# Prologue of a one-layer hybrid decoder: first loads on one queue in larger pieces, squares of x summed on GpSimd, the norm's product one group earlier

## The chip, the cores and the metric

The kernel runs on one core of one Trainium2 chip. The metric is the device time of one execution in microseconds. TensorE is called PE here, VectorE DVE, ScalarE ACT, GpSimd POOL and SyncE SP, as the profile does.

## The reference

One layer of a decoder trunk on x of 256 tokens by 1024 features, all float32:

```
xn   = rms_norm(x, attn_norm_g)              # x * rsqrt(mean(x*x) + eps) * g
proj = xn @ w_in                             # 1024 -> 3088 columns: q, k, v of 8 attention heads; q, k, v, r and a
                                             # 16-column gate of 4 gated-linear-attention heads
x    = x + concat(attention(rope(q), rope(k), v), gla(q', k', v', gate) * silu(r)) @ w_out
x    = x + ConvGLU(rms_norm(x))              # 1024 -> 2 x 2816, causal conv of 3 taps, silu gate, 2816 -> 1024
out  = rms_norm(x)
```

The first norm is what the change touches: the projection needs, for every token, one factor `rsqrt(mean(x*x) + eps)`.

## The kernel before, in words

x comes transposed, 128 features by 256 tokens in each of 8 k-tiles. Every float32 product is made of three reduced-precision ones: an operand is split into `hi` (rounded, by ACT, line 95) and `lo` (the rest, by DVE, line 98), and PE adds hi·hi, hi·lo and lo·hi. For x the two halves are `ah` (ACT, line 173) and `al` (DVE, line 174), multiplied with the norm's weight on the way; the norm's factor per token is left out and put in when a product is read back.

The projection runs in six groups of columns, "G" (gate and GLA q, k: 528 columns), then q, k, v, gv and r (512 each). A loop over q = 0 to 47 takes one k-tile of one group at a step: q 0 to 7 is group G, q 8 to 15 group q, and so on. In group G a step has three passes of four matmuls (line 671), with `hi,ah`, `hi,al` and `lo,ah`; in group q a step has 12 matmuls (lines 112 to 114). Everything else that ACT, DVE and SP do is hung on these steps by a table at line 587: the entry with number q is issued ahead of step q, one with q + 0.5 in its middle. On ACT, DVE and PE the order of issue is the order of the program; an instruction that waits holds all that stand behind it on its engine.

Weights come through four buffers `raw` ("slots"): slots 0 to 3 hold two k-tiles of group G each (`in_wG`, 528 KB a slot), slots 4 and 5 the two halves of group q (`in_w`, 1024 KB each, loaded in two pieces), and so on. When a slot's last `lo` is made, SP issues the load of the slot four further on. The kernel issues x in five pieces: k-tiles 0 and 1 from ACT's queue, 2-3, 4-5 and 6-7 from SP's, between the weights. A load takes one of eight completion semaphores in turn, and an issue waits until the load that had its semaphore before has landed.

The norm goes in these steps. `xsq(n)` squares two k-tiles (ACT, line 236). `xadd(n)` adds them up (DVE, line 239) and `xsum` makes one tile `s1` of 256 tokens (DVE, line 243). `xnorm` has PE sum `s1` over the partitions (line 250, ahead of the middle of step 8) and then makes the factor `rsx` with a Ln and an Exp on ACT (lines 181 and 182) and four small DVE instructions (lines 180 and 183 to 185). `g_evac` reads group G back with that factor (ACT, lines 266 and 267); `g_lr_split` splits its 16 gate columns (DVE, lines 278 and 279); `xrow` spreads the factor over a tile with PE (line 258) to scale cos and sin; `g_transpose_lr` and `g_transpose` transpose the read-back tiles on PE (lines 284 and 293).

Of the kernel before, what the change touches and what calls it, by code (L numbers as in the profile page):

```python
# [34 lines left out]
def trunk_kernel(ctx: ExitStack, tc: tile.TileContext, xT_d, wG_d, w5_d, wo_d, up_d, dn_d,  # L35
                 par_d, gla_g_d, fin_g_d, wgu_d, cos_d, sin_d, causal_d, lvl_d, ident_d, out_d):
    nc = tc.nc
# [13 lines left out]
        return ps_att.tile([128, 512], F32, name="att")  # L51


    par = const.tile([128, NPAR], F32, name="par")
    cos = const.tile([128, S], F32, name="cos")
    sin = const.tile([128, S], F32, name="sin")
# [91 lines left out]
    rsx = main.tile([128, 8], F32, name="rsx")  # L148

    slots[0].raw = ring.tile([128, 2048], F32, name="raw", bufs=RAW)  # L150
    def load_x(q, k0, k1):
        a, b = (KT + S * k0 if k0 else 0), KT + S * k1
        q.dma_start(xg[:, a:b], xT_d[:, a:b])


    with tc.manual_schedule(engines={mybir.EngineType.Activation}):
        load_x(A, 0, 1)
        load_x(A, 1, 2)
        A.preload_act_table_set("natural_log_exp_and_others")
    for a, b in ((0, 272), (272, NG), (NG, 2 * NG)):  # L160
        DMA.dma_start(slots[0].raw[:, a:b], slots[0].src[:, a:b])
    nload[0] = 1
    load_x(DMA, 2, 4)
    load_next()
    load_x(DMA, 4, 6)
    load_next()
    load_x(DMA, 6, 8)
    load_next()
    for dst, src in ((ident, ident_d), (cos, cos_d), (sin, sin_d), (par, par_d), (wgu, wgu_d)):
        DMA.dma_start(dst, src)  # L170
# [64 lines left out]
    def xsq(n):  # L235
        A.activation(xsqs[:, 2 * n:2 * n + 2], xT[:, 2 * n:2 * n + 2], AF.Square)

    def xadd(n):
        V.tensor_add(xsqs[:, 0:2], xsqs[:, 0:2], xsqs[:, 2 * n:2 * n + 2])

    def xsum():
        s1 = at.tile([128, S], F32, name="s1")
        V.tensor_add(s1, xsqs[:, 0], xsqs[:, 1])
        st["s1"] = s1
        st["mh"] = main.tile([128, KT, S], F32R, name="mh", tag="mh")

# [333 lines left out]
    def do(*fs):  # L580
        for f, *a in fs:
            f(*a)
# [1 line left out]


    for q, f in (
            (2, lambda: do((gsplit, 6), (xsq, 2), (xadd, 1), (gsplit, 7), (xsq, 3), (xadd, 2))),
            (4, lambda: do((hi, 4, 0), (lo, 4, 0), (xadd, 3), (xsum,), (hi, 4, 1), (lo, 4, 1))),
            (6, lambda: do((hi, 5, 0, 1),)),
            (8.5, lambda: do((xnorm,), (lo, 5, 0), (g_evac, 0), (g_evac, 1), (g_lr_split,), (hi, 6, 0), (lo, 5, 1))),  # L590
            (10, lambda: do((DMA.dma_start, lvl, lvl_d), (DMA.dma_start, causal, causal_d))),
            (10.5, lambda: do((xrow,), (g_wgs,))),
            (11, lambda: do((g_transpose_lr,), (g_transpose, 0), (g_transpose, 1), (lo, 6, 0), (g_diag,))),
            (12.5, lambda: do((g_gate_mm,), (g_gate,), (hi, 6, 1), (g_decay,), (lo, 6, 1), (hi, 7, 0))),
            (14, lambda: do((lvl_u, 0), (lo, 7, 0), (hi, 7, 1), (lvl_u, 1), (lo, 7, 1))),
            (16, lambda: do((rope_a, 0, 0), (rope_b, 0, 0), (rope_a, 0, 1), (rope_b, 0, 1), (hi, 8, 0), (lo, 8, 0), (hi, 8, 1), (lo, 8, 1))),
            (20, lambda: do((hi, 9, 0), (lo, 9, 0), (hi, 9, 1), (DMA.dma_start, glag, gla_g_d))),
            (24, lambda: do((lvl_first,), (lvl_u, 2), (rope_a, 1, 0), (rope_b, 1, 0), (rope_a, 1, 1), (rope_b, 1, 1), (lo, 9, 1), (hi, 10, 0), (lo, 10, 0), (g_diag2, 0), (g_diag2, 4))),
# [20 lines left out]
    def gsplit(k):  # L619
        sl, a = slots[k // 2], NG * (k % 2)  # L620
        if k % 2 == 0:
            sl.alloc()
        xsplit(k)
        if k == 1:
            xsq(0)
        sl.split(a, a + NG)

    slots[0].alloc()
# [4 lines left out]
    slots[0].split_lo(272, NG)  # L633
    for k in range(1, 5):
        gsplit(k)
    xsq(1)
    gsplit(5)

    def emit(q):
        for f, a in plan.get(q, []):  # L640
            f(*a)

    names = ["G", "q", "k", "v", "gv", "r"]
    for q in range(48):
        g, k = divmod(q, 8)
        emit(q)
        if k == 0:
            if g == 0:
                st["G"] = [(acc(), att()) for _ in range(2)]
            else:  # L650
                st[names[g]] = [acc() for _ in range(2)]
        if g == 0:
            h_, l_ = slots[k // 2].view(NG)
            kk = k % 2
        else:
            h_, l_ = slots[4 + 2 * (g - 1) + k // 4].view(512)
# [413 lines left out]
```

## Time and profile before

| | |
|---|---|
| median of 3 runs | 312.95 us (312.08 to 314.29) |
| profiled execution, its own time | 313.25 us |
| its span, first to last instruction | 311.3 us |
| PE busy | 303.0 us, 97% of the span |
| DVE, ACT, POOL busy | 79%, 65%, 1% of the span |
| DMA moved | 55.38 MB, mean 178 GB/s |
| mean granted TensorE clock | 0.996 |

The median is that of three timed runs; the profile is one more execution, whose time is 0.3 us above it. Busy time of PE says that matmuls are in flight; whether they follow each other without a gap is seen in the waits of PE and in the order of time.

### The profile page before, as it was taken

Reading aid. Unit: us, or ns where it says so; the run is one execution under the profiler, and the core shown is the slowest. Engines: PE = TensorE matmul, PEld = TensorE weight load, DVE = VectorE, ACT = ScalarE, POOL = GpSimd, SP = SyncE. Lnnn points to the kernel's source line nnn. Section 1 sums busy time; section 2 is a strip of 40 time slices with the busy share of each in tenths; the row PEclk is TensorE's granted clock in tenths of the full one; section 3 lists DMA queues with packets and bytes.
Section 4 is the critical chain, followed back from the end, with each engine's and each line's share of the span. In section 5 each row is a group of like instructions: output and inputs, shape, how many; then the busy total and the mean of one; then the engine's idle time right before and its main releaser. Section 6 shows DMA issues by size and latency. Waiting matters only on the chain.

```text
span 311.3 us, 6126 instructions
## 1 busy us (share of the span) xinstructions
PE 303.0 (97%) x2460; PEld 283.0 (91%) x2460; DVE 246.4 (79%) x455; ACT 201.0 (65%) x364; POOL 1.8 (1%) x12
## 2 busy tenths in 40 slices
PE   7999999999999999999999999999999999999992
PEld 7999997777789999999999999999999999999982
DVE  3879989988558497999999878788777777776653
ACT  5869997796967396467666655556666555534362
POOL 1000000000000000000000000000000000000000
PEclk9999999999999999999999999999999999999998
DMA  7998553543370725593566654445455722120003
GB/s 222 387 385 317 190 182 114 227 139 135 138 272 5 259 74 197 218 378 157 206 209 251 262 212 171 165 177 188 194 202 205 269 69 67 67 69 0 2 0 135
DMA packets 12155, 55.38 MB, mean 178 GB/s; under 512 B 1360, under 2 KB 2912, under 8 KB 7776
## 3 DMA queue, kind: packets, MB, share of 16 engines
q1 hardware_dynamic: 11696, 54.48, 47.9%
q10 hardware_dynamic: 432, 0.53, 0.6%
q8 instruction: 19, 0.31, 0.4%
q14 instruction: 8, 0.07, 0.1%
HBM read 53.95 MB, written 1.05 MB: 177 GB/s over the span
## 4 chain that ended last, share of the span: by engine, by line
PE 90%; DMA 6%; issue 1%; ACT 1%; DVE 1%; SPq 0%; DVEq 0%; ACTq 0%
PE att L114 14%; PE att L113 14%; PE att L112 14%; PE acc L112 14%; PE acc L113 14%; PE acc L114 14%; DMA raw<-in_w 2%; DMA raw<-in_wG 2%; DMA xg<-in_xT 1%; PE att L378 1%; PE att L541 1%; PE att L510 1%; PE att L556 1%; PE att L440 1%; PE acc L830 0%
## 5 line engine op out<-in xcount | busy, mean ns | idle before, releaser
L95 ACT ACTIVATE hi<-raw 128x1024 fp32r<-128x1024 f32 (+3 forms) x83 | 79.6, 977 | 52.2 <-PE att L113 43.1
L98 DVE TENSOR_TENSOR lo<-raw,hi 128x1024 fp32r<-128x1024 f32 (+3 forms) x86 | 93.8, 1099 | 11.9 <-ACT hi L95 11.8
L112 PE MATMUL att<-hh,hi 128*128 128x256 f32 x352 | 98.5, 280 | 0.0
L114 PE MATMUL att<-hh,lo 128*128 128x256 f32 x352 | 98.4, 279 | 0.0
L113 PE MATMUL att<-hl,hi 128*128 128x256 f32 x352 | 98.3, 279 | 0.0
L112 PEld LDWEIGHTS att<-hh,hi 128*128 128x128 f32 x352 | 66.2, 188 | 0.0
L114 PEld LDWEIGHTS att<-hh,lo 128*128 128x128 f32 x352 | 66.2, 188 | 0.0
L113 PEld LDWEIGHTS att<-hl,hi 128*128 128x128 f32 x352 | 66.2, 188 | 0.0
L796 DVE SCALAR_TENSOR_TENSOR c<-us,par,c 128x256 f32<-128x256 f32 x88 | 40.7, 482 | 4.1 <-ACT c L788 2.5
L788 ACT ACTIVATE c<-us,par 128x256 f32<-128x256 f32 x44 | 24.0, 591 | 21.6 <-DVE us L778 16.1
L114 PE MATMUL acc<-dhi,gl 128*128 128x512 f32 (+1 forms) x88 | 32.3, 367 | 0.0
L113 PE MATMUL acc<-dlo,gh 128*128 128x512 f32 (+1 forms) x88 | 32.2, 366 | 0.0
L112 PE MATMUL acc<-dhi,gh 128*128 128x512 f32 (+1 forms) x88 | 31.8, 361 | 0.0
L735 DVE TENSOR_TENSOR dlo<-draw,dhi 128x1024 fp32r<-128x1024 f32 x22 | 26.7, 1219 | 0.0
L778 DVE TENSOR_TENSOR us<-att,rb 128x512 f32<-128x512 f32 x20 | 13.8, 690 | 15.9 <-PE att L114 15.9
L730 ACT ACTIVATE dhi<-draw 128x1024 fp32r<-128x1024 f32 x22 | 23.1, 1049 | 0.0
L112 PE MATMUL acc<-hi,ah 128*128 128x512 f32 x48 | 19.8, 412 | 0.0
L113 PEld LDWEIGHTS acc<-dlo,gh 128*128 128x128 f32 x88 | 16.5, 188 | 2.9
L112 PEld LDWEIGHTS acc<-dhi,gh 128*128 128x128 f32 x88 | 16.6, 188 | 2.9
L114 PE MATMUL acc<-hi,al 128*128 128x512 f32 x48 | 19.0, 395 | 0.0
L113 PE MATMUL acc<-lo,ah 128*128 128x512 f32 x48 | 19.0, 395 | 0.0
L114 PEld LDWEIGHTS acc<-dhi,gl 128*128 128x128 f32 x88 | 16.5, 188 | 2.6
(208 smaller groups left out, 517.6 us busy)
## 6 DMA issues: line engine op xcount, KB each, us to landing
raw<-in_up SPq DMA_DIRECT2D x22, 1024.0 KB, 4.8
draw<-in_dn SPq DMA_DIRECT2D x22, 512.0 KB, 5.7
raw<-in_w SPq DMA_DIRECT2D x8, 1024.0 KB, 5.2
raw<-in_wo SPq DMA_DIRECT2D x4, 1024.0 KB, 4.8
raw<-in_w SPq DMA_DIRECT2D x4, 512.0 KB, 5.5
raw<-in_wG SPq DMA_DIRECT2D x3, 528.0 KB, 6.1
xg<-in_xT SPq DMA_DIRECT2D x3, 256.0 KB, 6.3
finb<-in_fin_g SPq DMA_DIRECT2D x1, 512.0 KB, 6.4
```

The source lines that it names most:

```text
L95: A.activation(self.hi[:, a:b], self.raw[:, a:b], AF.Copy)
L98: V.tensor_sub(self.lo[:, a:b], self.raw[:, a:b], self.hi[:, a:b])
L112: T.matmul(out, sh, mh, start=first, stop=False, **kw)
L113: T.matmul(out, sh, ml, start=False, stop=False, **kw)
L114: T.matmul(out, sl, mh, start=False, stop=last, **kw)
L378: T.matmul(p[h][64 * j:64 * j + 64, c + 32 * g:c + 32 * g + 32], k[ps, a:a + 64], q, start=True, stop=True)
L440: T.matmul(o, AT[:, i], gv[:, tt, vs], start=(tt == 0), stop=True)
L730: A.activation(hi, downs[i][0], AF.Copy)
L735: V.tensor_sub(lo, d, hi)
L778: V.tensor_tensor(u[:, :, 2:], upo[i][2].rearrange("p (a t) -> p a t", a=2), rb[:, None, :].to_broadcast([128, 2, S]), op=ALU.mult)
L788: A.activation(cv[i][:, a], u[:, a, 2:], AF.Identity, bias=par[:, P_CB + m:P_CB + m + 1], scale=par[:, P_CW + 2 * 2 * NP + m:P_CW + 2 * 2 ...
L796: V.scalar_tensor_tensor(c[:, a], u[:, a, w:w + S], par[:, wc:wc + 1], c[:, a], op0=ALU.mult, op1=ALU.add)
```

## The change

Four things are different. All first loads are issued by SP: x in pieces of 1, 3 and 4 k-tiles in place of 1, 1, 2, 2 and 2, the second k-tile of slot 0 behind the second piece of x, and the third piece of x ahead of slot 2. ACT issues no load, and its function table is loaded first. The sums of squares (`xadd`, `xsum`) are made by GpSimd in place of DVE; `xsq(1)` and `xsq(2)` stand elsewhere on ACT. `xnorm` stands inside the last step of group G, between its first and second pass. The read-back of group G stands ahead of the splits of slot 5, and `xrow` one step earlier.

```
+    A.preload_act_table_set("natural_log_exp_and_others")
...
-    with tc.manual_schedule(engines={mybir.EngineType.Activation}):
-        load_x(A, 0, 1)
-        load_x(A, 1, 2)
-        A.preload_act_table_set("natural_log_exp_and_others")
-    for a, b in ((0, 272), (272, NG), (NG, 2 * NG)):
+    load_x(0, 1)
+    for a, b in ((0, 272), (272, NG)):
         DMA.dma_start(slots[0].raw[:, a:b], slots[0].src[:, a:b])
+    load_x(1, 4)
+    DMA.dma_start(slots[0].raw[:, NG:2 * NG], slots[0].src[:, NG:])
     nload[0] = 1
-    load_x(DMA, 2, 4)
     load_next()
-    load_x(DMA, 4, 6)
+    load_x(4, 8)
     load_next()
-    load_x(DMA, 6, 8)
     load_next()
...
     def xadd(n):
-        V.tensor_add(xsqs[:, 0:2], xsqs[:, 0:2], xsqs[:, 2 * n:2 * n + 2])
+        nc.gpsimd.tensor_add(xsqs[:, 0:2], xsqs[:, 0:2], xsqs[:, 2 * n:2 * n + 2])
...
     def xsum():
+        for n in range(1, 4):
+            xadd(n)
         s1 = at.tile([128, S], F32, name="s1")
-        V.tensor_add(s1, xsqs[:, 0], xsqs[:, 1])
+        nc.gpsimd.tensor_add(s1, xsqs[:, 0], xsqs[:, 1])
...
-            (2, lambda: do((gsplit, 6), (xsq, 2), (xadd, 1), (gsplit, 7), (xsq, 3), (xadd, 2))),
-            (4, lambda: do((hi, 4, 0), (lo, 4, 0), (xadd, 3), (xsum,), (hi, 4, 1), (lo, 4, 1))),
-            (6, lambda: do((hi, 5, 0, 1),)),
-            (8.5, lambda: do((xnorm,), (lo, 5, 0), (g_evac, 0), (g_evac, 1), (g_lr_split,), (hi, 6, 0), (lo, 5, 1))),
+            (2, lambda: do((gsplit, 6), (xsq, 3), (gsplit, 7), (xsum,))),
+            (4, lambda: do((hi, 4, 0), (lo, 4, 0), (hi, 4, 1))),
+            (7.5, lambda: do((xnorm,),)),
+            (8, lambda: do((lo, 4, 1), (g_evac, 0), (g_evac, 1), (g_lr_split,), (hi, 5, 0), (lo, 5, 0))),
...
-            (10.5, lambda: do((xrow,), (g_wgs,))),
+            (9.5, lambda: do((xrow,), (g_wgs,), (hi, 5, 1), (hi, 6, 0), (lo, 5, 1))),
...
-        if k == 1:
-            xsq(0)
+        if k in (1, 3):
+            xsq(k // 2)
...
-    xsq(1)
+    xsq(2)
...
             for n, (mov, sta) in enumerate(((h_, ah), (h_, al), (l_, ah))):
+                if n == 1:
+                    emit(q + 0.5)
```

What this moves is best seen in the order of instructions. On ACT, from the last square of x to the first split behind the read-back of group G, there stood before (`hi` of slots 4 and 5 are the rows with 1024 columns, `rsx` is the norm's factor, `gqk` the read-back):

```order
L236 ACTIVATE xsqs<-xg 128x512
L95 ACTIVATE hi<-raw 128x1024 x4
L181 ACTIVATE rsx<-att,eps 128x2
L182 ACTIVATE rsx<-rsx 128x2
L266 ACTIVATE gqk<-acc,rsx 128x272
L267 ACTIVATE gqk<-att,rsx 128x256
L266 ACTIVATE gqk<-acc,rsx 128x272
L267 ACTIVATE gqk<-att,rsx 128x256
L95 ACTIVATE hi<-raw 128x1024
```

and there stands now (line numbers of the changed kernel):

```order
L233 ACTIVATE xsqs<-xg 128x512
L170 ACTIVATE ah<-xg 128x256
L96 ACTIVATE hi<-raw 128x528
L96 ACTIVATE hi<-raw 128x1024 x2
L178 ACTIVATE rsx<-att,eps 128x2
L179 ACTIVATE rsx<-rsx 128x2
L265 ACTIVATE gqk<-acc,rsx 128x272
L266 ACTIVATE gqk<-att,rsx 128x256
L265 ACTIVATE gqk<-acc,rsx 128x272
L266 ACTIVATE gqk<-att,rsx 128x256
L96 ACTIVATE hi<-raw 128x1024
```

The two splits of slot 5 moved from ahead of the factor to behind the read-back, and the last square moved ahead of the last split of x (`ah`) and of group G (`hi`, 528 columns).

On PE, at the seam of group G and group q, there stood before (`acc_333` and `acc_334` are the two accumulators of group q, `s1` the sum of squares):

```order
L112 MATMUL acc_333<-ah_95,hi_269 128x256
L113 MATMUL acc_333<-al_96,hi_269 128x256
L114 MATMUL acc_333<-ah_95,lo_270 128x256
L250 MATMUL att_341<-ones_80,s1_274 128x1 x2
L112 MATMUL acc_334<-ah_95,hi_269 128x256
```

and now, inside the last step of group G:

```order
L672 MATMUL acc_197<-hi_225,ah_96 128x272
L672 MATMUL acc_199<-hi_225,ah_96 128x272
L672 MATMUL att_198<-hi_225,ah_96 128x256
L672 MATMUL att_200<-hi_225,ah_96 128x256
L249 MATMUL att_313<-ones_81,s1_241 128x1 x2
L672 MATMUL acc_197<-hi_225,al_97 128x272
L672 MATMUL acc_199<-hi_225,al_97 128x272
```

The norm's product moved ahead by 14 matmuls: the 8 that group G still has, and 6 of group q.

On POOL, ahead of the memsets at the start of the second half (`us`), there stood before:

```order
L219 MEMSET ATf 64x8x64
L220 MEMSET wgs 128x256
L221 MEMSET lrs 128x256
L741 MEMSET us_1554 128x2x2
L741 MEMSET us_1555 128x2x2
```

and now:

```order
L216 MEMSET ATf 64x8x64
L217 MEMSET wgs 128x256
L218 MEMSET lrs 128x256
L236 ISA
L236 TENSOR_TENSOR xsqs<-xsqs 128x512 x3
L242 TENSOR_TENSOR s_241<-xsqs 128x256
L742 MEMSET us_1549 128x2x2
```

Four additions moved to POOL, and a new instruction ahead of them (ISA), which makes POOL's library ready and waits for nothing.

## Rows read from the trace of the kernel before

**Rows 1.** The page, busy time, share of the span and instructions of each engine.
```profile
PE 303.0 (97%) x2460; PEld 283.0 (91%) x2460; DVE 246.4 (79%) x455; ACT 201.0 (65%) x364; POOL 1.8 (1%) x12
```

**Rows 2.** Waits of PE, whole span: us in total, times, longest us.
```profile
PE att L284 <- DVE lrs L279: 0.5, 1, 0.5
PE att L258 <- issue: 0.4, 1, 0.4
```

**Rows 3.** PE in order of time, 22 to 26 us: start us, us, what [idle before].
```profile
22.39 0.28 PE L114 MATMUL acc<-ah,lo 128*128 128x256 f32 x1
23.05 0.68 PE L258 MATMUL att<-ident,rsx 128*128 128x128 f32 x4 [0.38 <-issue]
...
24.16 0.28 PE L114 MATMUL acc<-ah,lo 128*128 128x256 f32 x1
24.91 0.41 PE L284 MATMUL att<-ident,lrs 128*128 128x128 f32 x2 [0.47 <-DVE lrs L279]
```

**Rows 4.** The chain of waits, whole span: start us, us, what.
```profile
13.21 7.69 DMA raw<-in_w
```

**Rows 5.** ACT in order of time, 0 to 40 us.
```profile
1.65 1.28 ACT L159 ACT_TABLE_LOAD   x1 [1.65 <-PEq L1059]
4.61 0.51 ACT L173 ACTIVATE ah<-xg 128x256 fp32r<-128x256 f32 x1 [1.68 <-DMA xg<-in_xT]
...
7.29 0.51 ACT L173 ACTIVATE ah<-xg 128x256 fp32r<-128x256 f32 x1 [0.20 <-DMA xg<-in_xT]
...
9.22 0.49 ACT L173 ACTIVATE ah<-xg 128x256 fp32r<-128x256 f32 x1
...
10.71 0.65 ACT L95 ACTIVATE hi<-raw 128x528 fp32r<-128x528 f32 x1
...
13.65 0.62 ACT L236 ACTIVATE xsqs<-xg 128x512 f32<-128x512 f32 x1
14.17 0.50 ACT L173 ACTIVATE ah<-xg 128x256 fp32r<-128x256 f32 x1
...
15.10 0.62 ACT L236 ACTIVATE xsqs<-xg 128x512 f32<-128x512 f32 x1
...
20.92 1.06 ACT L95 ACTIVATE hi<-raw 128x1024 fp32r<-128x1024 f32 x1 [1.15 <-DMA raw<-in_w]
21.88 0.24 ACT L181 ACTIVATE rsx<-att,eps 128x2 f32<-128x2 f32 x1
...
22.98 0.49 ACT L266 ACTIVATE gqk<-acc,rsx 128x272 f32<-128x272 f32 x1 [0.62 <-DVE rsx L185]
```

**Rows 6.** DVE in order of time, 0 to 40 us.
```profile
4.35 0.30 DVE L629 CAST hi<-raw 128x272 fp32r<-128x272 f32 x1 [3.36 <-DMA raw<-in_wG]
...
14.48 0.68 DVE L239 TENSOR_TENSOR xsqs<-xsqs 128x512 f32<-128x512 f32 x1
...
16.70 1.22 DVE L98 TENSOR_TENSOR lo<-raw,hi 128x1024 fp32r<-128x1024 f32 x1
...
18.56 0.42 DVE L243 TENSOR_TENSOR s<-xsqs 128x256 f32<-128x256 f32 x1
```

**Rows 7.** Waits of ACT, whole span: us in total, times, longest us.
```profile
ACT hi L95 <- PE att L113: 43.1, 14, 4.0
```

**Rows 8.** PE in order of time, 12 to 32 us: the last step's second pass.
```profile
17.56 0.41 PE L671 MATMUL acc<-hi,al 128*128 128x272 f32 x2
```

**Rows 9.** Windows, steps 0 and 2: busy PE, PEld, DVE, ACT, POOL, PEclk, DMA, GB/s.
```profile
5.17:7.83 2.66, 2.66 (x12) 2.65 (x12) 2.26 (x5) 2.38 (x5) 0.00 (x0) 1.00 1.01 356
...
9.66:11.12 1.46, 1.46 (x15) 1.46 (x13) 1.46 (x4) 1.41 (x4) 0.00 (x0) 1.00 1.06 410
```

**Rows 10.** POOL in order of time, whole span.
```profile
1.03 0.52 POOL L219 MEMSET ATf<- 64x512 f32 x1
...
1.86 0.30 POOL L221 MEMSET lrs<- 128x256 f32 x1
```

**Rows 11.** The page, DMA issues: count, KB each, median us to landing.
```profile
raw<-in_wG SPq DMA_DIRECT2D x3, 528.0 KB, 6.1
```

More of the change, by code (lines that the diff above doesn't have):

```diff
@@ L150, in trunk_kernel, with load_x @@
     slots[0].raw = ring.tile([128, 2048], F32, name="raw", bufs=RAW)
-    def load_x(q, k0, k1):
+    def load_x(k0, k1):
         a, b = (KT + S * k0 if k0 else 0), KT + S * k1
-        q.dma_start(xg[:, a:b], xT_d[:, a:b])
-    with tc.manual_schedule(engines={mybir.EngineType.Activation}):
-        load_x(A, 0, 1)
-        load_x(A, 1, 2)
-        A.preload_act_table_set("natural_log_exp_and_others")
-    for a, b in ((0, 272), (272, NG), (NG, 2 * NG)):
+        DMA.dma_start(xg[:, a:b], xT_d[:, a:b])
+    load_x(0, 1)
+    for a, b in ((0, 272), (272, NG)):
         DMA.dma_start(slots[0].raw[:, a:b], slots[0].src[:, a:b])
+    load_x(1, 4)
+    DMA.dma_start(slots[0].raw[:, NG:2 * NG], slots[0].src[:, NG:])
     nload[0] = 1
-    load_x(DMA, 2, 4)
     load_next()
-    load_x(DMA, 4, 6)
+    load_x(4, 8)
     load_next()
-    load_x(DMA, 6, 8)
     load_next()
@@ L586, in trunk_kernel @@
     for q, f in (
-            (2, lambda: do((gsplit, 6), (xsq, 2), (xadd, 1), (gsplit, 7), (xsq, 3), (xadd, 2))),
-            (4, lambda: do((hi, 4, 0), (lo, 4, 0), (xadd, 3), (xsum,), (hi, 4, 1), (lo, 4, 1))),
-            (6, lambda: do((hi, 5, 0, 1),)),
-            (8.5, lambda: do((xnorm,), (lo, 5, 0), (g_evac, 0), (g_evac, 1), (g_lr_split,), (hi, 6, 0), (lo, 5, 1))),
+            (2, lambda: do((gsplit, 6), (xsq, 3), (gsplit, 7), (xsum,))),
+            (4, lambda: do((hi, 4, 0), (lo, 4, 0), (hi, 4, 1))),
+            (7.5, lambda: do((xnorm,),)),
+            (8, lambda: do((lo, 4, 1), (g_evac, 0), (g_evac, 1), (g_lr_split,), (hi, 5, 0), (lo, 5, 0))),
             (10, lambda: do((DMA.dma_start, lvl, lvl_d), (DMA.dma_start, causal, causal_d))),
-            (10.5, lambda: do((xrow,), (g_wgs,))),
+            (9.5, lambda: do((xrow,), (g_wgs,), (hi, 5, 1), (hi, 6, 0), (lo, 5, 1))),
             (11, lambda: do((g_transpose_lr,), (g_transpose, 0), (g_transpose, 1), (lo, 6, 0), (g_diag,))),
             (12.5, lambda: do((g_gate_mm,), (g_gate,), (hi, 6, 1), (g_decay,), (lo, 6, 1), (hi, 7, 0))),
-            (14, lambda: do((lvl_u, 0), (lo, 7, 0), (hi, 7, 1), (lvl_u, 1), (lo, 7, 1))),
+            (14.5, lambda: do((lvl_u, 0), (lo, 7, 0), (hi, 7, 1), (lvl_u, 1), (lo, 7, 1))),
             (16, lambda: do((rope_a, 0, 0), (rope_b, 0, 0), (rope_a, 0, 1), (rope_b, 0, 1), (hi, 8, 0), (lo, 8, 0), (hi, 8, 1), (lo, 8, 1))),
```

## The prediction

> **What bounds the kernel now.** I read the busy shares first, then the waits of PE, PE itself in order of time, the chain of waits, and ACT and DVE in order of time. PE is busy for 303.0 of 311.3 us [rows 1], so a change gains only where PE stands still. Between PE's first projection matmul and the end of the last group the waits of PE name only two stops, both between 22 and 25 us [rows 2]. In order of time they are larger than the idle time printed [rows 3]: matmuls of 256 columns start 0.117 us apart there, so after the one that starts at 22.39 the next could have started at 22.51, and L258 starts at 23.05: 0.54 us lost. After 24.16 the next could have started at 24.28, and L284 starts at 24.91: 0.63 us lost. Together 1.17 us.
>
> The chain shows what is behind them: a load of slot 5 that is in flight from 13.21 for 7.69 us [rows 4]. ACT's split of it starts at 20.92 after 1.15 us of waiting for the load, and the norm's Ln stands behind it at 21.88 [rows 5], although the sum of squares had been ready since 18.98 (18.56 + 0.42, [rows 6]). So the factor is late because of its place on ACT, and PE waits for what the factor gives: first `xrow`, then the transposes. Later ACT waits for PE and not the reverse: its splits for 43.1 us [rows 7]. Time that PE gains at 25 us should therefore last to the end.
>
> **The change part by part.** *The norm's place.* ACT's Ln no longer stands behind slot 5, so the load that landed at 20.9 does not matter to it. In the new order the factor needs: the last square, two sums on POOL, the product on PE, a small DVE instruction behind the first split of slot 4, then Ln, Exp and three small DVE instructions. PE comes to the product just ahead of the pass that started at 17.56 [rows 8]; the split of slot 4 was done at 17.92 (16.70 + 1.22, [rows 6]); I take 18.1. So Ln comes near 18.3. From Ln to the read-back took 1.10 us (21.88 to 22.98, [rows 5]): read-back from 19.4. From there to the transposes' start took 1.93 (22.98 to 24.91, [rows 3]): ready at 21.3. PE ends group G eight matmuls (0.122 each, a twelfth of 1.46, [rows 9]) and one product after 17.56; with 0.5 us for the product (as for `xrow`: 23.05 to 24.16 less five matmuls, [rows 3]) that is 19.0. `xrow` comes 18 matmuls later, at 21.1, and the transposes at 23.7. Both have what they need, with some 2 us to spare. **Both stops go: 1.17 us.** The products themselves only change places: nothing.
>
> *The loads.* PE's first projection matmul waited for x's first k-tile, which was there at 4.61 and split by 5.12 [rows 5]; the first weights had been there at 4.35 [rows 6]. Now this piece of x is alone at the head of the one queue. So the first matmul can be up to 0.5 us earlier (4.35 + 0.30 = 4.65 against 5.17). But step 1 needs `hi` of the second k-tile, and that load now stands behind three more k-tiles of x. The same 1044 KB lay ahead of what ACT got at 7.29 [rows 5]; with 0.63 us for the split step 1 starts near 7.9, against 7.83 before [rows 9]. If the large piece of x lands only 0.66 us ahead of it (264 KB at 410 GB/s, [rows 9]), ACT has a split and a square to do first, and step 1 starts at 8.2. Bounds: 0.55 us gained (weights at 7.0, step 1 at 7.65 and at once at the later pace) to 0.4 us lost. I take 0: early x is worth nothing while step 1 waits for the same bytes. The third piece of x now lies whole ahead of slot 2, which lands 0.64 us later (262 kB at 410 GB/s): its split starts near 11.35 instead of 10.71 [rows 5] and ends at 12.0; PE wants it for step 4, at 9.66 + 2 x 1.46 = 12.58 [rows 9]. Covered, with 0.6 us left.
>
> *The squares.* From that split to the end of the last square took 5.01 us before (10.71 to 15.72). The last pair of splits (0.93, 14.17 to 15.10) now comes behind that square and one other square (0.52, 13.65 to 14.17) ahead [rows 5]: 3.56 us, so the last square is done at 14.9. DVE loses 3 x 0.68 + 0.42 = 2.46 us of additions [rows 6], which gives its later splits room and PE nothing.
>
> *The sums on POOL.* The trace has no addition on POOL, only memsets: 0.52 us for 512 elements and 0.30 for 256 [rows 10], one stream written. An addition reads two streams and writes one. Lower bound one stream (0.52 and 0.30), upper bound three one after the other (1.56 and 0.90); I take two, 1.04 and 0.60: DVE's 0.68 lies between, and two reads of one memory are the nearest. The first two sums are out of the way by then (their squares end at 9.22 + 0.40 + 0.62 = 10.2 and at 12.5). So `s1` is there at 14.9 + 1.64 = 16.5 (bounds 15.7 to 17.4), and PE asks for it at 17.56. No wait at either bound: 0.
>
> *The new POOL instruction* that makes the library ready waits for nothing and can begin at 2.2 us [rows 10], 8 us before the first sum has its input. The nearest one-off load in the trace is ACT's table, 1.28 us [rows 5]; a common transfer took 6.1 us to land [rows 11]. Either is over by 8.3: 0.
>
> **Sum:** 313.25 - 1.17 = 312.1 us for the profiled execution. That execution stands 0.3 above the median of 312.95, so against the median the forecast is **311.8 us**. The three runs spread over 2.2 us; less than about 1% can't be told from no change here.
>
> **Rivals.** *An earlier start (faster).* If k-tile 1 lands at 7.0 and PE goes at the later pace at once, the start gives 0.55 us on top: 311.25. Step 0 took 2.66 us and step 2 took 1.46, both at a granted clock of 1.00, the 2.4 GHz level [rows 9], so that column does not explain the slow pace, and a start without the pause before it may move the point where it ends. For it: x's first load was the gate. Against it: the bytes of step 1.
>
> *POOL and DVE hold each other up.* DVE is busy without a gap from 9.66 to 11.12 [rows 9], and its splits read two tiles of SBUF, as the sums do. If only one of the two engines can do so at a time, a sum waits for the DVE instruction in front: some 0.7 us for the third sum and 1.22 [rows 6] for `s1`. Then `s1` is there at 14.9 + 0.7 + 1.04 + 1.22 + 0.60 = 18.5, PE stands 0.9 us at the product, and 0.25 us of gain is left: 312.7. DVE is held up by two sums (2.1 us) ahead of the last split of group G and has one addition less there (0.68); its lead was about 2 us (the pass that needs it started four matmuls after 17.56, at 18.05, and DVE had done it and an addition by 16.70), so this costs no more. No row before has both engines at SBUF reads. The Trainium skill, "SBUF — State Buffer", section "Who interferes with whom", states just this: a DVE instruction with two SBUF inputs contends with a GpSimd instruction that reads SBUF, and the later one blocks. By that rule this rival would be the likeliest; no run here shows it yet.
>
> *The library comes late (slower than before).* If POOL's code is fetched not at the new instruction but when the first sum is called, the delay L counts from 10.2, and `s1` is there at 10.2 + L + 3 x 1.04 + 0.60 = 13.9 + L. Up to L = 3.6 nothing is lost; from L = 4.8 on, the wait at the product is more than 1.17 us and the kernel is slower than before. With L as long as the transfer above, 6.1 us, `s1` comes at 20.0, PE stands for 2.5 us, and the time is 312.95 + 1.3 = 314.3. For it: transfers of that length are common here. Against it: the instruction stands 8 us ahead. The Trainium skill, "GPSIMD Engine Reference", section "2.1 Instruction dispatch", states that the first call to a freshly loaded kernel pays about 6 us for this load; counted from the call that would make 314.2, counted from the new instruction it is hidden, and no row here tells which.
>
> *The gain is given back.* If some later work of DVE or ACT has less than 1.2 us of lead on PE, PE waits there instead: 312.95. Against it: ACT waits for PE again and again [rows 7].
>
> **How the numbers follow.** Forecast (both stops gone, no new wait, 311.4 to 312.2): 0.45. Earlier start, 310.6 to 311.4: 0.15. Shared access, 312.2 to 312.9: 0.22. Late library, 313.5 to 315: 0.10. Given back, about 313: 0.08. The range of 310.5 to 313.4 leaves out the late library and about 0.08 at its ends. A gain of over 1% (below 309.8) needs more than all the stops that PE has: 0.03. A loss of over 1% (above 316.1) needs a library that is 8 us late: 0.03. Within 1%: 0.94.
>
> **What would show it.** Right: no idle time before `xrow` and the transposes (L257, L283 in the changed kernel), the Ln near 18.3, no wait of PE at the norm's product (L249), additions on POOL of about 1.04 us, step 1 of group G at 7.7 to 8.0. Shared access: a wait at L249 of 0.3 to 1 us, and POOL or DVE instructions longer than the others of their kind. Late library: POOL's first sum long after its square. The forecast is wrong if PE is 1 us ahead at 30 us but not at 300, or if the start moves by more than 0.5 us.

## The result, and the profile after

The changed kernel takes 315.67 us (median of 8 runs, 314.87 to 316.58) against 313.21 us of the kernel before in the same comparison: 1.0081 times as long, interval 1.0064 to 1.0099. It is slower by 2.5 us where 1.2 us less was forecast. The profiled execution took 316.34 us, 0.7 us above the median of its kernel; its span is 314.2 us (before 311.3).

The page's busy times of the changed kernel, to be held against [rows 1]:

```profile
PE 303.6 (97%) x2460; PEld 284.0 (90%) x2460; DVE 247.4 (79%) x451; ACT 200.9 (64%) x364; POOL 6.9 (2%) x16
```

POOL has gained 5.1 us of additions. DVE's busy time has risen by 1.0 us although it has four additions (2.46 us) less to make; the rest has hardly changed. The page alone does not say where 2.9 us of span went. The waits of PE up to 40 us do (in total, times, longest):

```profile
PE acc L672 <- ACT hi L96: 3.8, 1, 3.8
PE att L75 <- DVE warm L70: 1.1, 1, 1.1
```

Both lines of [rows 2] are gone, and one wait of 3.8 us has come: for the first split weights of step 1. PE in order of time shows both, with the places that answer to [rows 3] and [rows 8] (L249 is the norm's product, L257 `xrow`, L283 the first transposes):

```profile
4.12 0.79 PE L672 MATMUL acc<-hi,ah 128*128 128x272 f32 x2
...
5.74 0.40 PE L672 MATMUL att<-lo,ah 128*128 128x256 f32 x2
9.94 0.82 PE L672 MATMUL acc<-hi,ah 128*128 128x272 f32 x2 [3.80 <-ACT hi L96]
...
12.74 0.66 PE L672 MATMUL acc<-hi,ah 128*128 128x272 f32 x2
...
15.23 0.41 PE L672 MATMUL acc<-hi,ah 128*128 128x272 f32 x2
...
21.34 0.40 PE L672 MATMUL att<-hi,ah 128*128 128x256 f32 x2
21.57 0.50 PE L249 MATMUL att<-ones,s 128*128 128x1 f32 x4
...
24.99 0.27 PE L115 MATMUL acc<-ah,lo 128*128 128x256 f32 x1
25.11 0.60 PE L257 MATMUL att<-ident,rsx 128*128 128x128 f32 x4
...
27.54 0.28 PE L115 MATMUL acc<-ah,lo 128*128 128x256 f32 x1
27.66 0.38 PE L283 MATMUL att<-ident,lrs 128*128 128x128 f32 x2
```

The first projection matmul comes at 4.12, 1.05 us earlier than before, and step 0 is over by 6.14. Then PE stands until 9.94. In the kernel before, steps 1, 2 and 3 began at these places:

```profile
8.04 0.66 PE L671 MATMUL acc<-hi,ah 128*128 128x272 f32 x2
...
9.78 0.41 PE L671 MATMUL acc<-hi,ah 128*128 128x272 f32 x2
...
11.24 0.41 PE L671 MATMUL acc<-hi,ah 128*128 128x272 f32 x2
```

(The prediction took 7.83 and 9.66 for steps 1 and 2, from the edges of its windows.) Steps 1 and 2 take 2.80 and 2.49 us now (before 1.74 and 1.46), so step 3 begins at 15.23 instead of 11.24. Behind it there is no stop: at 21.57, 25.11 and 27.66 each matmul starts when the one ahead of it has been issued.

What PE stood for is in the chain of waits (start, us, what):

```profile
1.63 0.42 SPq L158
...
2.09 6.21 DMA xg<-in_xT
...
8.33 0.51 ACT ah L170
8.84 0.52 ACT xsqs L233
9.35 0.54 ACT hi L96
```

The DMA at its head is the 384 KB piece with k-tiles 1 to 3 of x; it takes the part that the load of slot 5 had in [rows 4]. ACT shows both ends of it, and the factor's Ln and the read-back, which answer to [rows 5]:

```profile
8.33 0.51 ACT L170 ACTIVATE ah<-xg 128x256 fp32r<-128x256 f32 x1 [3.90 <-DMA xg<-in_xT]
8.74 0.61 ACT L233 ACTIVATE xsqs<-xg 128x512 f32<-128x512 f32 x1
9.26 0.63 ACT L96 ACTIVATE hi<-raw 128x528 fp32r<-128x528 f32 x1
...
22.37 0.26 ACT L178 ACTIVATE rsx<-att,eps 128x2 f32<-128x2 f32 x1 [2.73 <-DVE rsx L177]
...
23.54 0.49 ACT L265 ACTIVATE gqk<-acc,rsx 128x272 f32<-128x272 f32 x1 [0.68 <-DVE rsx L182]
```

ACT has nothing to do for 3.90 us, and the Ln waits for the product now, not for slot 5. Windows of one microsecond show the loads and the clock (busy PE, PEld, DVE, ACT, POOL, then PEclk, DMA share, GB/s):

```profile
4.00:5.00 1.00, 1.00 (x6) 1.00 (x6) 1.00 (x3) 0.42 (x1) 0.00 (x0) 1.00 0.79 188
5.00:6.00 1.00, 1.00 (x10) 0.93 (x8) 0.06 (x1) 0.00 (x0) 0.00 (x0) 1.00 1.01 230
6.00:7.00 1.00, 0.14 (x2) 0.00 (x0) 0.00 (x0) 0.00 (x0) 0.00 (x0) 1.00 0.65 201
7.00:8.00 1.00, 0.00 (x0) 0.00 (x0) 0.00 (x0) 0.00 (x0) 0.00 (x0) 1.00 1.05 374
8.00:9.00 1.00, 0.00 (x0) 0.00 (x0) 0.13 (x1) 0.67 (x2) 0.00 (x0) 0.61 1.03 420
9.00:10.00 1.00, 0.06 (x1) 0.06 (x1) 0.43 (x2) 1.00 (x3) 0.00 (x0) 0.50 1.01 412
...
14.00:15.00 1.00, 1.00 (x7) 1.00 (x6) 1.00 (x4) 1.00 (x3) 0.43 (x1) 0.50 0.94 313
15.00:16.00 1.00, 1.00 (x10) 1.00 (x10) 1.00 (x2) 1.00 (x3) 1.00 (x1) 0.98 0.88 293
```

From 4 to 7 us the one queue brings 188 to 230 GB/s. The kernel before had 307 to 349 in the same microseconds:

```profile
4.00:5.00 1.00, 0.40 (x2) 0.11 (x1) 0.30 (x1) 0.39 (x1) 0.00 (x0) 1.00 1.04 307
5.00:6.00 1.00, 0.83 (x3) 0.82 (x4) 0.85 (x3) 0.90 (x4) 0.00 (x0) 1.00 0.97 347
6.00:7.00 1.00, 1.00 (x6) 1.00 (x6) 0.72 (x2) 1.00 (x3) 0.00 (x0) 1.00 1.04 349
```

And while PE stands still, from 6.14 to 9.94, its granted clock falls: 0.61 from 8 to 9 us, then 0.50, the 1.2 GHz level, until 15 us. Steps 1 and 2 run at that level. The page's DMA list tells the same of slots 1 to 3: 6.1 us from issue to landing in [rows 11], now

```profile
raw<-in_wG SPq DMA_DIRECT2D x3, 528.0 KB, 9.2
```

POOL's additions and DVE's splits, in order of time, POOL first:

```profile
12.20 1.27 POOL L236 TENSOR_TENSOR xsqs<-xsqs 128x512 f32<-128x512 f32 x1 [10.04 <-ACT xsqs L233]
14.57 1.64 POOL L236 TENSOR_TENSOR xsqs<-xsqs 128x512 f32<-128x512 f32 x1 [1.09 <-ACT xsqs L233]
...
18.35 0.81 POOL L242 TENSOR_TENSOR s<-xsqs 128x256 f32<-128x256 f32 x1
```

```profile
12.69 1.35 DVE L99 TENSOR_TENSOR lo<-raw,hi 128x528 fp32r<-128x528 f32 x1 [0.35 <-ACT hi L96]
...
14.36 0.69 DVE L99 TENSOR_TENSOR lo<-raw,hi 128x528 fp32r<-128x528 f32 x1
14.98 1.51 DVE L171 SCALAR_TENSOR_TENSOR al<-xg,ah 128x256 fp32r<-128x256 f32 x1
```

An addition takes 1.27 to 1.64 us and the last one 0.81; a DVE split that meets one takes 1.35 instead of 0.69, or 1.51 instead of 0.48 (256 columns). The two long splits end behind the additions that they meet (14.04 against 13.47, 16.49 against 16.21), and the longest addition is the one that begins inside a split (14.57; that split ends at 15.05). The sum is there at 19.16 and PE asks for it at 21.57, so here it costs PE nothing.

### The profile page after: what moved, and what is told of

It reads as the page before. It is cut to its first block, busy times and chain, and to the rows that moved or that the text cites. A ratio compares the mean times of both kernels' runs of the same rounds, so it can differ in the third digit from the quotient of the medians.

```text
span 314.2 us, 6128 instructions
## 1 busy us (share of the span) xinstructions
PE 303.6 (97%) x2460; PEld 284.0 (90%) x2460; DVE 247.4 (79%) x451; ACT 200.9 (64%) x364; POOL 6.9 (2%) x16
## 3 DMA queue, kind: packets, MB, share of 16 engines
HBM read 53.95 MB, written 1.05 MB: 175 GB/s over the span
## 4 chain that ended last, share of the span: by engine, by line
PE 95%; DMA 2%; ACT 1%; SPq 0%; DVE 0%; issue 0%; DVEq 0%; ACTq 0%
PE acc L113 14%; PE acc L115 14%; PE acc L114 14%; PE att L113 14%; PE att L114 14%; PE att L115 14%; PE acc L672 2%; DMA xg<-in_xT 2%; PE att L672 2%; PE att L377 1%; PE att L540 1%; PE att L509 1%; PE att L555 1%; PE att L439 1%; PE acc L831 0%; PE att L437 0%
```

## The experiments

**One table for all runs.** From the product of the gate (`g_gate_mm`, the matmul `att<-lrT,wgs`) to the end, every profiled execution below takes 283.2 to 283.5 us. So each difference lies ahead of that product (the changed kernel and those built from it also issue the work of step 14 half a step later, which stands behind it). Three stretches of PE's order of time divide the time ahead of it: the start of step 3 of group G (how late the loads and the clock make it), step 3 to step 7 (5.84 us if nothing stops PE), and step 7 to the gate's product (the norm: 11.05 us with the two stops of before, 9.77 without). Ratios are to the kernel before in the same comparison (its medians there lie between 313.21 and 313.54), with their intervals; they are not quotients of the medians in the table.

| run | step 3 at | 3 to 7 | 7 to gate | gate at | median us | ratio |
|---|---|---|---|---|---|---|
| before | 11.24 | 5.84 | 11.05 | 28.13 | 313.21 | |
| changed | 15.23 | 5.86 | 9.77 | 30.86 | 315.67 | 1.0081 [1.0064, 1.0099] |
| e1 sums on DVE | 14.29 | 5.83 | 9.76 | 29.88 | 315.63 | 1.0078 [1.0057, 1.0100] |
| e2 sums on POOL alone | 10.90 | 5.98 | 11.35 | 28.23 | 313.39 | 1.0002 [0.9992, 1.0012] |
| e3 norm's place alone | 10.77 | 5.83 | 10.94 | 27.54 | 313.01 | 0.9988 [0.9976, 0.9999] |
| e4 PE kept busy | 13.34 | 7.25 | 9.78 | 30.37 | 314.78 | 1.0049 [1.0031, 1.0067] |
| e5 old loads | 11.44 | 7.62 | 9.78 | 28.84 | 313.20 | 0.9998 [0.9986, 1.0010] |
| e6 two queues, large | 12.20 | 6.23 | 9.77 | 28.20 | 313.45 | 1.0008 [0.9996, 1.0020] |
| e7 one queue, small | 11.72 | 7.62 | 9.76 | 29.10 | 314.55 | 1.0039 [1.0027, 1.0052] |
| e8 one queue, x cut | 14.57 | 6.04 | 9.76 | 30.37 | 314.94 | 1.0056 [1.0034, 1.0078] |
| e9 norm ahead of slot 5 | 11.77 | 5.83 | 10.68 | 28.28 | 313.67 | 1.0011 [1.0001, 1.0020] |
| e10 old loads, three sums out | 11.19 | 5.86 | 9.77 | 26.82 | 311.87 | 0.9952 [0.9939, 0.9965] |
| e11 slot 1 ahead | 15.84 | 5.82 | 9.77 | 31.43 | 316.92 | 1.0110 [1.0089, 1.0131] |
| e12 loads dealt anew | 10.91 | 5.84 | 11.23 | 27.98 | 313.38 | 1.0004 [0.9992, 1.0016] |
| e13 norm ahead, gate in time | 11.43 | 5.82 | 10.30 | 27.55 | 312.91 | 0.9977 [0.9961, 0.9992] |
| e14 e13, loads dealt anew | 10.83 | 5.83 | 10.99 | 27.65 | 312.63 | 0.9973 [0.9959, 0.9988] |
| e15 changed, three sums out | 13.59 | 5.82 | 9.77 | 29.18 | 315.11 | 1.0054 [1.0032, 1.0077] |

The stretches are of one execution each. The column "step 3 at" varies by 1 us without any change of the loads (10.77 to 11.77 with those of before) and by 1.6 us with the changed ones (13.59 in e15, 14.29 in e1, 15.23), so where it matters the ratios decide.

**e1, the sums back on DVE, loads as changed** (is it POOL, or the fetching of its library, that delays the loads?).

```
-        nc.gpsimd.tensor_add(xsqs[:, 0:2], xsqs[:, 0:2], xsqs[:, 2 * n:2 * n + 2])
+        V.tensor_add(xsqs[:, 0:2], xsqs[:, 0:2], xsqs[:, 2 * n:2 * n + 2])
```

> The changed kernel with the four sums of squares back on DVE (the first two as soon as their squares are there), so that POOL has no addition and no instruction that makes its library ready; loads and the norm's place as in the change. Theory L (POOL's library is fetched over the DMA engines from 2.2 us on and slows the first loads): the large piece of x lands near 6.3 us instead of 8.3, step 1 starts at 7.9 or before, PE's granted clock stays at 1.00, time 311.2 to 312.5. Theory Q (one queue with large pieces is slow by itself): x lands at 8.3 again, the clock falls again, time 315.5 or a little more.

The same time as the changed kernel, and PE again waits 3.7 us ahead of step 1. Without any addition on POOL the loads are as late: they are the cause, not POOL.

**e2, only the sums moved to POOL** (the kernel before otherwise).

```
-        V.tensor_add(s1, xsqs[:, 0], xsqs[:, 1])
+        nc.gpsimd.tensor_add(s1, xsqs[:, 0], xsqs[:, 1])
```

> The kernel before with nothing changed but the four sums on POOL. Theory L: x's pieces and the weights of the first steps land 1 to 2 us later than before although they are issued as before, steps 1 to 3 start late, time 314.5 to 317. Theory Q: the loads land as before, the factor comes no later than before, time 312.7 to 313.7.

No change that can be measured. PE did not have the two stops of before in this execution; it waited 0.4 and 0.2 us for DVE's `lo` and 0.2 us for its `al` instead, came to `xrow` at 23.88 (before 23.05), and found the factor ready.

**e3, only the norm's new place** (loads of before, sums on DVE; the squares and the splits stand as in the changed kernel).

```
-            (8.5, lambda: do((xnorm,), (lo, 5, 0), ...
+            (7.5, lambda: do((xnorm,),)),
+            (8, lambda: do((lo, 4, 1), (g_evac, 0), ...
```

> The changed kernel with the loads of the kernel before (two pieces of x from ACT's queue, five pieces in all) and the sums on DVE: what is left of the change is the norm's place. Both theories: the loads land as in the kernel before, both stops of PE before xrow and the transposes are gone (1.17 us), at most 0.4 us is lost at the norm's product: 311.7 to 312.6 against 313.2.

Both stops go, and PE waits 0.9 us at the norm's product for the sum that DVE makes too late for it. What is left is a tenth of a per cent: the new place needs the sums earlier than DVE has them.

**e4, 14 warming products between steps 0 and 1** of the changed kernel (what does the fall of the clock cost?).

```
+        if q == 1:
+            warming(14, 128)
```

> The changed kernel with 14 more warming products of 128 columns on PE (their result is not used) between steps 0 and 1, where PE stood for 3.8 us. If the fall of the granted clock to one half is what the pause costs beyond itself: step 1 starts at 9.9 as in the changed kernel, steps 1 and 2 take 1.46 us each and not 2.64, step 3 starts near 12.9 and not 15.2, time 315.7 - 2.3 = 313.4. If the clock has another cause or the data of steps 1 to 3 set their pace: 315.0 to 315.9.

The granted clock stays at 1.00 and step 3 comes at 13.34 instead of 15.23, 1.9 us earlier, but the time falls by only 0.9 us, to a value between the two expectations. The table shows where the rest went: from step 3 to step 7 PE now needs 7.25 us. Its waits there are for DVE's `lo` and `al`. With the clock kept up, PE gets to the splits that POOL's sums hold up. One of the eight executions of the changed kernel had a mean granted clock of 0.997, about as before, and took 315.58 us all the same. What the fall of the clock alone costs is therefore not shown; keeping it up gave back 0.9 us here.

**e5, the loads of before, all else as changed.**

```
-    load_x(1, 4)
-    DMA.dma_start(slots[0].raw[:, NG:2 * NG], slots[0].src[:, NG:])
+    with tc.manual_schedule(engines={mybir.EngineType.Activation}):
+        load_x(A, 0, 1)
+        load_x(A, 1, 2)
```

> The whole change but for the first loads, which are those of the kernel before (two queues, its pieces, its order). If the loads alone made the kernel slower: both stops stay gone (no wait before the norm's row and the transposes), no wait at the norm's product because the sums on POOL are ready at about 19.2 or before, step 1 of the first group near 7.8, and 311.9 to 312.3 us, 1.0 to 1.3 below the kernel before. If something else in the change costs time (POOL's sums holding DVE up, the new order of the splits): 313.3 or more.

313.20 us, and not the 312 that I expected. Step 3 comes at 11.44, so the loads are what made it late; the norm's stretch is 9.78, so its gain is real; but steps 3 to 7 take 7.62 us. DVE in order of time:

```profile
11.31 1.37 DVE L98 TENSOR_TENSOR lo<-raw,hi 128x528 fp32r<-128x528 f32 x1 [0.35 <-ACT hi L95]
...
13.00 1.80 DVE L98 TENSOR_TENSOR lo<-raw,hi 128x528 fp32r<-128x528 f32 x1
...
15.73 1.52 DVE L174 SCALAR_TENSOR_TENSOR al<-xg,ah 128x256 fp32r<-128x256 f32 x1
17.18 1.24 DVE L98 TENSOR_TENSOR lo<-raw,hi 128x528 fp32r<-128x528 f32 x1
```

POOL, beside it:

```profile
10.83 1.29 POOL L239 TENSOR_TENSOR xsqs<-xsqs 128x512 f32<-128x512 f32 x1 [8.66 <-ACT xsqs L236]
12.88 1.34 POOL L239 TENSOR_TENSOR xsqs<-xsqs 128x512 f32<-128x512 f32 x1 [0.77 <-ACT xsqs L236]
15.27 1.71 POOL L239 TENSOR_TENSOR xsqs<-xsqs 128x512 f32<-128x512 f32 x1 [1.04 <-ACT xsqs L236]
17.05 0.80 POOL L245 TENSOR_TENSOR s<-xsqs 128x256 f32<-128x256 f32 x1
```

And PE:

```profile
14.85 0.52 PE L675 MATMUL acc<-lo,ah 128*128 128x272 f32 x2 [0.38 <-DVE lo L98]
...
18.47 0.52 PE L675 MATMUL acc<-lo,ah 128*128 128x272 f32 x2 [0.41 <-DVE lo L98]
```

Each of these four splits lies beside one POOL addition. Together they are 3.4 us longer than such splits alone (1.37 + 1.80 + 1.52 + 1.24 less three of 0.70 and one of 0.48), more than the 2.46 us of additions that DVE was spared. So the late loads had hidden a second loss.

**e6, two queues, pieces as large as changed**; **e7, one queue, pieces small and in the order of use**; **e8, one queue, the changed order, the 384 KB piece cut in three.**

```
e6:  +        load_x(A, 0, 1)
     +        load_x(A, 1, 4)
e7:  +    load_x(DMA, 1, 2)
     +    DMA.dma_start(slots[0].raw[:, NG:2 * NG], slots[0].src[:, NG:])
     ...
     +    load_x(DMA, 2, 4)
e8:  -    load_x(1, 4)
     +    for k in range(1, 4):
     +        load_x(k, k + 1)
```

> The changed kernel with x's first two pieces (k-tile 0, then k-tiles 1 to 3 in one) issued by ACT's queue beside SP's, all sizes as in the change. Theory queue (one queue moves the first megabyte slowly): the large piece lands at about 6.5, step 1 starts by 8.2, no fall of the clock, 312.0 to 312.6 us. Theory size (a piece is usable only when its last byte is there, and the large one is late in any queue): it lands at 8 or later, step 1 starts at 9 or later, 314.5 to 315.7 us.

> The changed kernel with all first loads on SP's queue still, but in small pieces in the order in which they are used: k-tile 0, first weights in two, k-tile 1, second weights, k-tiles 2 to 3, slot 1, 4 to 5, slot 2, 6 to 7, slot 3. Theory queue: the bytes up to the second weights (784 KB) are as many as those that came at 8.3 in the changed kernel, so the second weights land at about 8.3, step 1 starts at 9 to 9.3, 314 to 315 us. Theory size and order: k-tile 1 at about 6 and the second weights at about 7, step 1 at 7.5 to 8.2, 311.8 to 312.6 us.

> The changed kernel with its own order on the one queue, and only the piece of k-tiles 1 to 3 cut into three of 128 KB. Theory queue: the same bytes lie ahead of the second weights, which land at about 9.2 as before the cut; step 1 starts at 9.7 or later, 315 to 316 us. Theory order (two k-tiles that are not needed yet lie ahead of the second weights): as the queue theory here. Theory size: the smaller pieces spread better, the second weights land by 7.5, step 1 by 8.2, 312.0 to 312.8 us.

With e5 and the changed kernel, e6 and e7 make a square. Two queues: 0.9998 with small pieces, 1.0008 with large ones, no difference beyond the intervals. One queue: 1.0039 with small pieces in the order of use, 1.0081 with the large ones. So the one queue costs 0.41% with small pieces and 0.73% with large ones, and size and order cost 0.42% on the one queue and nothing that can be told on two. e8 lies between (its interval overlaps both neighbours, and its step 1, at 9.12, stands between the theories' 8.2 and 9.7). Neither theory alone holds: the queue brings fewer bytes, and then what stands first in it decides. e6 missed the 312.0 to 312.6 of the queue theory too: its step 3 comes at 12.20, and steps 3 to 7 take 6.23 us. Bytes from 2 to 9 us, in e6 and in e7:

```profile
2.00:9.00 7.00, 6.07 (x27) 5.45 (x26) 3.06 (x7) 4.21 (x8) 0.16 (x1) 1.00 0.98 333
```

```profile
2.00:9.00 7.00, 6.14 (x36) 5.72 (x34) 3.06 (x7) 3.01 (x7) 0.17 (x1) 1.00 0.93 260
```

The last two figures of a row are the DMA share and GB/s. The other kernels with two queues have 306 GB/s there (e5) to 324 (e3, e12), the kernel before 316; those with one have 263 (e8), 266 (changed), 268 (e4), 286 (e15), 287 (e1) and 288 (e11). Issuing does not explain the rate: SP takes 0.43 us for an issue, and the last of the 1044 KB up to the second weights is issued at 3.00 us in the changed kernel (2.57 + 0.43), the same amount at 2.53 before (2.10 + 0.43), while the rates differ from 4 to 7 us. Nor is it likely to be ACT's function table, whose place goes with the number of queues in these runs: in the changed kernel it is loaded by 2.01 us (0.73 + 1.28).

In one point my expectation for e7 was wrong: step 1 began at 6.96, since k-tile 1 stood fourth in the queue and had landed by 5.35; PE waited up to 1.5 us for `hi` later instead. The two profiles of e5 and e7 differ by only 0.3 us of span; e5's profiled execution was the slowest of its ten (313.82), so for this pair the medians are to be read.

**e11, slot 1 ahead of the second weights and of the 384 KB piece** (is the one queue slow at its start, or on short rows?).

```
     nload[0] = 1
     load_next()
+    DMA.dma_start(slots[0].raw[:, NG:2 * NG], slots[0].src[:, NG:])
+    load_x(1, 4)
```

> The changed kernel on its one queue, with the order of three loads turned: after the first weights come slot 1 (rows of 4.2 KB), the second weights (2.1 KB), and then the piece of k-tiles 1 to 3 (3 KB). Theory start (one queue moves little in its first 5 us, whatever it carries): about 200 GB/s from 4 to 7 us as in the changed kernel, 370 or more when the piece of x goes. Theory rows (one queue is slow on rows of 3 KB and less): 300 GB/s or more from 4 to 6 us, then about 200 while the second weights and x go. Either way step 1 starts at 9.5 to 11 and the time is 316 to 318 us.

The rates are 224 GB/s from 4 to 5 us, 347 from 5 to 6, then 323 to 326 from 6 to 8 while the piece of x went. Longer rows came faster in the microsecond where the changed kernel had 230, but x was not slow later. Neither theory is borne out; why one queue brings less here stays open.

**e9, the splits of slot 5 moved behind the norm, nothing else** of the kernel before; **e10, the kernel of e5 with three of the four sums left out** (its factor comes from two of the eight squares); **e12, e9 with the first loads dealt to the two queues the other way round.**

```
e9:  -            (6, lambda: do((hi, 5, 0, 1),)),
     +            (8.5, lambda: do((xnorm,), (g_evac, 0), (g_evac, 1), (g_lr_split,), (hi, 5, 0), ...
e10: -        for n in range(1, 4):
     -            xadd(n)
e12: +        load_g0(A, 0, 272)
     +        load_x(A, 1, 2)
     ...
     +    load_x(DMA, 0, 1)
```

> The kernel before (its loads, its sums on DVE, the norm's product where it was) with one thing moved: the two splits of slot 5 on ACT stand behind the norm's Ln and the read-back of G, not in front. Theory that both stops of PE come from Ln's place behind slot 5: no idle time before the norm's row and the transposes, Ln near 20, and 1.0 to 1.2 us less than before, 312.0 to 312.4 us. Rival, that the gain is given back later or that slot 5 is then split too late for PE: a new wait of PE for the split of slot 5 of 0.5 us or more, or the same time as before, 313.2 to 313.6 us.

> The whole change with the first loads of the kernel before, as run already, and the three larger sums on POOL left out (the factor is then computed from two of the eight squares). Theory that POOL's sums hold DVE's splits up and so PE: DVE's splits take 0.71 and 0.48 again but for one, PE's waits for DVE's lo go, and the time falls by 0.8 to 1.3 us against the same kernel with the sums (313.2), to 311.9 to 312.4. Rival, that the new order of the splits or the place of the product costs what the norm gains: no change, 313.0 to 313.5 us.

> The kernel before with the splits of slot 5 behind the norm, as in the run beside it, and the first loads dealt to the two queues the other way: SyncE's has k-tile 0 of x in front and ACT's the first half of the first weights, then k-tile 1; all pieces as small as before. Theory that the start is set by when x and weights are both there, and that two queues are enough: first projection matmul at 4.2 to 4.7 (before 5.17), step 1 at 7.0 to 7.8, no wait of over 0.5 us in steps 1 and 2, 311.3 to 312.2 us. Rival, that an earlier start only moves the wait to the later steps, whose loads come no earlier: waits of PE for hi at steps 1 and 2 of together 0.5 to 1.5 us, and the same time as the run beside it, 312.0 to 312.5 us.

e10 is the plain case: without the three additions no split of group G on DVE takes over 0.71 us but the one beside the sum that is left (0.81), steps 3 to 7 take 5.86, and the time is 311.87 us. That is 1.3 us below e5. It is what the change would have given if the loads and the sums had cost nothing. That it meets the forecast of 311.8 is in part luck: against the kernel before beside it e10 is 0.48% faster (interval 0.35 to 0.61%), 1.5 us, and 1.17 were forecast. In e9 the two stops go, and a new one comes, among PE's waits:

```profile
PE att L316 <- DVE wgs L273: 0.7, 1, 0.7
```

Between the read-back and the gate's weights `wgs` ACT now has three splits, where it had one. The rival of its expectation held: what is gained is given back later.

e10 also has an early call of POOL. The one sum that is left needs only the first square, which ends at 6.13 (5.52 + 0.61):

```profile
6.21 0.73 POOL L243 TENSOR_TENSOR s<-xsqs 128x256 f32<-128x256 f32 x1 [4.05 <-ACT xsqs L236]
```

In e12 PE's first projection matmul comes 0.4 us sooner than before (4.74), and the same new wait is there, of 1.0 us.

**e13, e9 with the gate's weights split first**; **e14, the same with the loads of e12**; **e15, the changed kernel with the same three sums left out.**

```
e13, e14: +            (10.5, lambda: do((xrow,), (g_wgs,), (hi, 5, 1), (lo, 5, 1), (hi, 6, 0))),
e15:      -        for n in range(1, 4):
          -            xadd(n)
```

> The kernel before (loads, sums on DVE, place of the product as before) with the splits of slot 5 behind the norm, and now the second of them and slot 6's behind the split of the gate's weights, so that the gate's product does not wait as it did in the run with only the first move. Theory that PE's two stops are real time: no idle time before the norm's row, the transposes and the gate's product, the last at 27.1 to 27.6 where the start is that of before, and 1.0 to 1.3 us less than before: 312.0 to 312.4 us. Rival, that whatever is gained here is given back by a later wait: a wait of 0.5 us or more that was not there, 313.0 to 313.6 us.

> As the run beside it, with the first loads dealt to two queues as in the earlier run (SyncE's has k-tile 0 in front, ACT's the first half of the first weights and k-tile 1). From that earlier run's start (0.3 us ahead at step 3) less the wait before the gate's product: 0.2 to 0.4 us below the run beside it, 311.7 to 312.1 us. Rival, that the start comes out the same in the median: no difference within 0.1%.

> The changed kernel with its own loads and the three larger sums on POOL left out (the factor is computed from two of the eight squares). Theory that the late loads cover POOL's cost to DVE: no change against the changed kernel, 315.4 to 315.9 us, so that the loads alone cost about 3.7 us against the kernel without both (311.87). Rival, that the two costs add up: 1.3 us less, 314.2 to 314.6 us.

e13 is faster than before by 0.23% (interval 0.08 to 0.39%), 0.7 us, and not by 1.0 to 1.3: its stretch from step 7 to the gate is 10.30, 0.75 below before. It has 0.2 us of standstill at the gate's product and comes 0.25 us later to the norm's product. e14 waits 0.4 us at the norm's product for the sum on DVE; it is the fastest kernel that leaves nothing out, 312.63 us, 0.27% below before (0.12 to 0.41%); against e13 the difference lies within the intervals. e15 falls between its two expectations (315.11), with executions from 312.66 to 316.50; whether the sums cost anything under the late loads is not settled by it.

## Why the prediction was wrong

**The loads: the step that failed.** "I take 0: early x is worth nothing while step 1 waits for the same bytes", with bounds of 0.55 gained and 0.4 lost. In the profiled execution the term is +4.0 us at step 3 (15.23 against 11.24), in two parts: step 1 starts 1.9 us later (9.94 against 8.04), and steps 1 and 2 take 2.1 us more (5.29 against 3.20) at a granted clock of 0.50, which had fallen while PE stood. That execution is one of the slower ones. In medians, with the rest alike, the new loads cost 0.83% (changed against e5), 0.90% (e1 against e3) and 1.02% (e15 against e10): 2.6 to 3.2 us. The error has two halves, as the square shows. One was to count bytes ahead and take the rate from [rows 5] and [rows 9], which are of two queues (356 and 410 GB/s): the same 1044 KB came at 188 to 230 GB/s for three microseconds (0.41% with small pieces). The other was to price the size and order of the pieces at 0.4 us at most: k-tile 1, which step 1 needs, was usable only with the whole 384 KB piece, at 8.30, while alone and fourth in the queue it was there by 5.35 (e7; 0.42%). With the term put in, the sum for the profiled executions is 313.25 - 1.17 + 4.0 = 316.1, measured were 316.34; in medians it is 313.21 - 1.17 + 3.2 = 315.2 against 315.67, with 0.4 us left that the intervals cover. The prediction's own sign of being wrong, a start that moves by more than 0.5 us, came.

**The early x.** k-tile 0 did come sooner (first matmul at 4.12, below the 4.65 of the forecast). PE also reached its later pace inside step 0, as the rival of an earlier start held possible: the last pair of matmuls of step 0 starts 1.62 us behind its first (5.74), before it was 2.45. Neither was worth anything: step 0 was over by 6.14, and the time gained became standstill, in which the clock fell.

**The norm's place: right.** Both stops are gone, there is no wait at L249, and the stretch from step 7 to the gate is 1.28 us shorter in the changed kernel, against 1.17 forecast. The Ln came 4.1 us later than the 18.3 forecast (22.37), which is the 4.0 of the late start. The estimate for the squares held too: 3.56 us from slot 2's split to the end of the last square, only from 13.25 on and not from 11.35. e13 shows part of the gain, 0.7 us, in a kernel that leaves nothing out.

**The sums on POOL: the rival of shared access was right, and in this kernel its cost is hidden.** They took 1.27 to 1.64 and 0.81 us against estimates of 1.04 and 0.60 and upper bounds of 1.56 and 0.90. The rival priced the loss at 0.9 us, at the norm's product, and held DVE's lead to be enough. In e5 the place was another: PE stops at DVE's `lo` in steps 4 and 6, and the four steps from 3 to 7 take 1.78 us more. e10 shows that these go with the sums. In the changed kernel PE is 4 us late, so DVE is in time: with the sums on DVE (e1) the time is the same, and e4 brings the waits out. e15 leaves open whether something of the cost remains. The Trainium skill, "SBUF — State Buffer", section "Who interferes with whom", states that a DVE instruction with two SBUF inputs contends with a GpSimd instruction that reads SBUF; this trace agrees (1.51 us instead of 0.48, 1.35 instead of 0.69).

**The library: not late.** The first sum starts at 12.20; its square, which started at 11.51 and took 0.61 us, ended at 12.12. The Trainium skill, "GPSIMD Engine Reference", section "2.1 Instruction dispatch", has about 6 us at the first call to a freshly loaded kernel; no such wait stands ahead of the call here. In e10, where the call comes early, the sum starts at 6.21, at once behind its square and 4.0 us after POOL's last memset (2.16): whatever was loaded was there by then. Whether an earlier execution had left it there is not shown.

**The gain given back: not seen here.** From the gate's product to the end the changed kernel takes 283.3 us, before 283.2: what happens at 28 us lasts to the end, as the prediction had it.

**Range and chances.** 315.67 lies 2.3 us above the range. The loss of 0.8% is inside the 1% that the prediction allowed with a chance of 0.94, but its sign was not forecast. No rival had the loads late: the one on the slower side priced the library. A bound of the rate from a row with one queue was missing.

## What to carry to other kernels

Bytes ahead of a load give its time only at the rate of the same queues: moving early loads to one queue is a change of rate, to be bounded by a row with one queue, or by the slowest row, and not by the mean of two queues. A large piece is usable only when its last byte is there. A first piece that comes earlier is worth nothing if the second comes later; while PE stands still between them, its clock may fall as well. A gain hidden behind a delay, and a loss hidden behind it, both come out only when the delay is taken away, so divide the time ahead of the first point that all runs share into stretches and compare those.

## What the runs showed of the hardware

One queue brought 260 to 288 GB/s from 2 to 9 us (seven kernels) where two brought 306 to 333 (ten kernels), although the same single queue brings 374 to 420 from 7 to 10 us in the changed kernel; why is open. The granted clock fell to 0.61 and then 0.50 while PE stood from 6.14 to 9.94, and was back at 0.98 in the window from 15 us, with PE busy since 9.94; with 14 small products in the gap it stayed at 1.00 (e4). PE's pace differs at a granted clock of 1.00 too: the changed kernel, with PE busy from 1.05 us without a pause, started pairs of matmuls of step 0 every 0.24 to 0.25 us from 5.00 on; the kernel before, after a pause of 0.77 us, took 2.87 us for the six pairs of its step 0 (5.17 to 8.04). An addition of 512 columns takes 0.68 us on DVE [rows 6] and 1.27 to 1.77 on POOL (eight kernels), and a DVE split of 528 columns beside one took up to 1.80 us instead of 0.70 (e5).
